# Loading the conditioning vector first, and two gate feature tiles beside the second chunk's norm

## The chip, the cores and the metric

The kernel runs on one core of a Trainium2 chip. Times are microseconds (us) of the device for one execution of the whole program. The names of the engines follow the profile: PE is TensorE (matmuls and transposes), PEld its weight loads, DVE is VectorE, ACT is ScalarE, POOL is GpSimd, and SP (SPq in the rows) is the queue from which every DMA of this kernel is issued.

## The reference

Two layers of a transformer-like block work on 1024 latent tokens and 256 context tokens of width 1024, all in float32. What matters here is the beginning of each layer:

```
shift, scale, gate = split(silu(c) @ w_mod[l] + b_mod[l], 3)        # latent; the context has its own from c_ctx
h  = rms_norm(x, norm_gain[l]) * (1 + scale) + shift
hc = rms_norm(ctx, norm_gain[l]) * (1 + scale_c) + shift_c
aq, ak, av, ag, bz, bg, nq, nk, nv, ng = split(h @ w_in[l], ...)     # widths 512,128,128,512,256,256,256,256,256,256
y = concat([attention(aq, ak, av) * silu(ag),
            pooling(bz) * silu(bg),
            neighbourhood_attention(nq, nk, nv) * silu(ng)]) @ w_out[l]
x = x + gate * y
```

The vector `c` and the learned vector `c_ctx` give, through the modulation weights `w_mod`, a shift and a scale for every one of the 1024 features. Only with these can a row of `x`, once normalized, be made into `h`, and only `h` can be multiplied by `w_in`. `ag` is the gate of the large attention: 512 features, that is four feature tiles of 128.

## The kernel before, in words

**Tiles.** Tokens come in chunks: tokens 0 to 511, 512 to 1023, and the 256 context tokens. `h` is kept transposed (features on the partitions) as a sum of a rounded part and a rest, `hh` and `hl`, each 128 x 8 x 1280. Weights are split in the same way into `wh` and `wl`, so one product of a 128-feature block takes three matmuls (hi by hi, hi by lo, lo by hi), and a feature tile of 512 tokens takes 8 x 3 = 24 matmuls (`feat_step`, L423 to L428; `proj_feat`, L430).

**The steps of a chunk.** `h_norm` (L234) squares the rows of a chunk on ScalarE, forms 1/rms, and scales the rows on VectorE. The squares themselves are of no use (only their sums are), and are written to a place that is free at the time: columns of `hl` that belong to the context, at L241. `h_steps` (L263) then gives eight steps, one for each block of 128 features: PE transposes up to four 128 x 128 tiles into a PSUM bank, ScalarE applies scale and shift and writes `hh`, GpSimd subtracts the shift again, and VectorE writes the rest to `hl`, reading the same bank. The steps lie in a list, `todo`, and `fill(n)` issues the next n of them at the place where it is called.

**Banks.** Three banks, `ps_b`, are handed out in turn by `ps_one` (L125): to the steps, to the small products of the modulation, and to some feature tiles. One bank, `ps_c`, is for the modulation rows. Four more, `ps_w`, hold the accumulators of feature tiles in this stage.

**The opening of layer 0.** The order of the DMAs is: identity and mask, the four row tiles of the first chunk (`x0`, L305, 512 KB each), the small rows of `c`, `c_ctx`, norm gain and modulation bias (`vrow`, L309), a selection matrix, and the first block of modulation weights (`mod_load`, L313, two transfers of 512 KB). Then comes a loop over j (L514). In round j, as far as j allows, the weight tile of the pooling branch for block j (256 KB) and the modulation weights of block j+1 are loaded; in rounds 2 to 5 also one row tile of the second chunk (`x1`, L519). PE computes the modulation of block j (`mod_rows`, L321), the columns of block j-1 (`mod_set`, L331), the first chunk's step for block j-1, and, three rounds behind, the four feature tiles of the pooling branch for block j-3. In rounds 4 to 7 the second chunk's rows are squared, and in round 7 scaled; its steps are issued two at a time in the last rounds, as are the loads and the norm of the context.

**Behind the loop.** The first chunk's four feature tiles leave their banks (`pool_in`), the second chunk's four tiles are computed with up to three context steps behind each of them (L564 to L567; the fourth takes its accumulator from `ps_one`), then the context chunk's tiles. The stages for the other columns of `w_in` follow, and last before the attention the gate stage (L716 to L740 and L805): weights of `ag`, two tiles for the context, and eight feature tiles (four features by two chunks), each multiplied with its SiLU (`silu_to`: three ScalarE passes and one VectorE product) and stored to `agd` in DRAM, from where the attention fetches it much later.

**What sets the order.** TensorE's instructions run in the order of the code. The order on the other engines and on the DMA queue is laid by the framework from the dependences; every wait on a buffer or a bank is set by it too.

Of the kernel before, what the change touches and what calls it, by code (L numbers as in the profile page):

```python
# [7 lines left out]
F32 = mybir.dt.float32  # L8
F32R = mybir.dt.float32r
BF16 = mybir.dt.bfloat16  # L10
AF = mybir.ActivationFunctionType
# [5 lines left out]
P = 128  # L17
D = 1024
# [56 lines left out]
def hybrid_block_kernel(  # L75
# [46 lines left out]

    ps_pair = ps_bank = ps_wide

    def ps_one(name):  # L125
        wide.b += 1
        return ps_b[wide.b % 3]

    def ps_acc(name):
        return ps_c  # L130
# [100 lines left out]
    def rows3(t):  # L231
        return t.rearrange("p (k c) -> p k c", c=P)

    def h_norm(n, hp=None):  # L234

        ss = small.tile([P, 4], F32, tag="lnss", name="lnss")
        xts, outs = [], []

        def add(xt):

            o = rows3(hp.tile([P, D], F32, name="xn", bufs=4)) if hp else hl[:, :, NTL * P:(NTL + 1) * P]  # L241
            i = len(xts)
            xts.append(xt)
            outs.append(o if hp else xt)
            ACT.activation(out=o, in_=xt, func=AF.Square, accum_out=ss[:, i:i + 1])

        def done():
            vv = small.tile([P, 4], F32, tag="lnv", name="lnv")
            DVE.tensor_scalar(out=vv[:, :n], in0=ss[:, :n], scalar1=1.0 / D, scalar2=EPS, op0=ALU.mult, op1=ALU.add)
            y = rsqrt(vv[:, :n], n, "ln")  # L250
            for i, xt in enumerate(xts):
                DVE.tensor_scalar(out=outs[i], in0=xt, scalar1=y[:, i:i + 1], scalar2=None, op0=ALU.mult)
            return outs

        return add, done

    def h_norm_all(xts):
        add, done = h_norm(len(xts))
        for xt in xts:
            add(xt)  # L260
        return done()

    def h_steps(l, t0, xns, hp, tname="htmp"):  # L263
        n = len(xns)
        v = 0 if t0 < NTL else 1
        w = n * P

        def step(k):
            ps = ps_one("ps_ht")
            for i in range(n):  # L270
                PE.transpose(ps[:, i * P:(i + 1) * P], xns[i][:, k, :], ident)
            a, b, nb = acol[:, l, v, k:k + 1], bcol[:, l, v, k:k + 1], nbcol[:, l, v, k:k + 1]
            dst = hh[:, k, t0 * P:t0 * P + w]
            ACT.activation(out=dst, in_=ps[:, :w], func=AF.Identity, scale=a, bias=b)
            tmp = hp.tile([P, 512], F32, name=tname, bufs=2)
            POOL.tensor_scalar(out=tmp[:, :w], in0=dst.bitcast(F32), scalar1=1.0, scalar2=nb, op0=ALU.mult, op1=ALU.add)
            DVE.scalar_tensor_tensor(out=hl[:, k, t0 * P:t0 * P + w], in0=ps[:, :w], scalar=a, in1=tmp[:, :w],
                                     op0=ALU.mult, op1=ALU.subtract)

        return [lambda k=k: step(k) for k in range(KT)]  # L280
# [19 lines left out]
    def load_x(t0, n, tiles):  # L300
        for i, xt in enumerate(tiles):
            SP.dma_start(out=xt, in_=rows3(x_rows(t0 + i)))
        return tiles

    x0 = load_x(0, 4, [rows3(pm.tile([P, D], F32, name="xt", bufs=8)) for _ in range(4)])  # L305
    vrow = pm.tile([40, P], F32, name="vrow")
    for r, v in ((0, c[0]), (8, c_ctx), (16, norm_gain[0]), (24, b_mod[0, 0:2 * D])):
        v = v.rearrange("(k p) -> k p", p=P)
# [4 lines left out]
    def mod_load(j):  # L313

        blk = stg.tile([P, KT, 256], F32, name="wmod", bufs=4)
        for i in range(2):
            SP.dma_start(out=blk[:, :, i * P:(i + 1) * P],
                         in_=w_mod[0, :, i * D + j * P:i * D + (j + 1) * P].rearrange("(k p) c -> p k c", p=P))
        return blk
# [18 lines left out]
        DVE.tensor_scalar(out=nbcol[:, 0, :, j], in0=bcol[:, 0, :, j], scalar1=-1.0, scalar2=None, op0=ALU.mult)  # L338

    blocks = [mod_load(0)]  # L340
    ps = ps_one("ps_v")
    PE.transpose(ps[:, 0:40], vrow, ident[0:40, 0:40])
    vcol = pm.tile([P, 40], F32, name="vcol")
# [30 lines left out]
    for l in range(DEPTH):  # L374
# [16 lines left out]
        def fill(n=1):  # L391
            for _ in range(n):
                if todo:
                    todo.pop(0)()

        def load_w_tile(cols, k):

            wh = wp.tile([P, 512], F32R, name="wh", bufs=9)
            wl = wp.tile([P, 512], F32R, name="wl", bufs=9)
            raw = wp.tile([P, 512], F32, name="wraw", bufs=4)  # L400
            o = 0
            for c0, w in cols:
                SP.dma_start(out=raw[:, o:o + w], in_=w_in[l, k * P:(k + 1) * P, c0:c0 + w])
                o += w
            split_w((wh, wl), raw[:, :o], slice(0, o))
            return wh, wl
# [30 lines left out]
        def silu_to(dst, ps, n, s=None):  # L437
            s = s or wp.tile([P, 512], F32, name="sig", bufs=2)
            sigmoid(s[:, :n], ps)
            DVE.tensor_tensor(out=dst, in0=ps, in1=s[:, :n], op=ALU.mult)  # L440


        ntok = SEQ if last else NT
        L = ntok + (24 if last else 32)
# [44 lines left out]
        if l:  # L489

            W = early_w + [load_w_tile([(C_BZ, 512)], k) for k in range(2, KT)]
            banks = []
            for i in range(2):
                pr = ps_pair("ps_feat")
                banks += [pr[:, 0:512], pr[:, 512:1024]]
            for i in range(2):
                for k in range(2):
                    for f in (2 * i, 2 * i + 1):
                        feat_step(banks[f], W, k, f, 0, 512)
            for k in range(2, KT):  # L500
                for f in range(4):
                    feat_step(banks[f], W, k, f, 0, 512)
                if k > 3:
                    fill(2)
            oprx.close()
            prex.close()
            W[:2] = [load_w_tile([(C_BZ, 512)], k) for k in range(2)]
        else:
            W = []

            banks = [ps_bank("ps_feat") for _ in range(4)]
            rows = None
            x1 = [rows3(pm.tile([P, D], F32, name="xt", bufs=8)) for _ in range(4)]
            for j in range(KT + 4):  # L514
                if j < KT:
                    W.append(load_w_tile([(C_BZ, 512)], j))
                    if j + 1 < KT:
                        blocks.append(mod_load(j + 1))
                    if 2 <= j < 6:  # L519
                        load_x(2 + j, 1, x1[j - 2:j - 1])  # L520
                    nxt = mod_rows(blocks[j])
                if 1 <= j <= KT:
                    mod_set(j - 1, rows)
                    first_h[j - 1]()
                if j == 4:
                    add1, done1 = h_norm(4)
                if 4 <= j < 8:
                    add1(x1[j - 4])
                if j == 7:
                    todo += h_steps(0, 4, done1(), wp, "sig")  # L530
                if j == KT:
                    SP.dma_start(out=edge, in_=k_edge)
                    x2 = load_x(NTL, 2, [rows3(pm.tile([P, D], F32, name="xt", bufs=8)) for _ in range(2)])
                if j == KT + 2:
                    todo += h_steps(0, NTL, h_norm_all(x2), wp, "sig")
                rows = nxt
                if j > KT:
                    fill(2)
                if 3 <= j < KT + 3:
                    for f in range(4):  # L540
                        feat_step(banks[f], W, j - 3, f, 0, 512)
            stx.close()
        lay = ExitStack()
        lp = lay.enter_context(pool(f"lay{l}", side=left))
        if l:
# [12 lines left out]
            DVE.memset(zt[:, :, 24 + NT:32 + NT], 0.0)  # L558
        for f in range(2):
            pool_in(f, 0, 512, banks[f])  # L560
        fill(2)
        for f in range(2, 4):
            pool_in(f, 0, 512, banks[f])
        for t0, n in chunks[1:2]:  # L564
            for f in range(4):
                pool_in(f, t0, n, proj_feat(W, f, t0, n, ps_one if l or f == 3 else None))
                fill(3)  # L567
# [8 lines left out]
        if l:  # L576
            use_banks("one")
        if l == 0:
            pmx.close()
            modp = pmx.enter_context(pool("modp", side="right"))  # L580
            todo += mod_part(0, 2 * D, modp, 2)
            for c0 in (0, D, 2 * D):
                todo += mod_part(1, c0, modp, 2)
            todo.append(lambda: mod_cols(1))
# [139 lines left out]
            silu_to(g, ps, 512)  # L724
            SP.dma_start(out=agc[t - NTL], in_=g)

        def gate_out(ps, f, t0, n, s=None):
            g = s or wp.tile([P, 512], F32, name="gate", bufs=2)
            silu_to(g, ps, 512, s)
            SP.dma_start(out=agd[f, :, t0:t0 + n], in_=g)  # L730

        def gate_feat(f, t0, n):
            gate_out(proj_feat(W, f, t0, n, ps_one if f == 3 else None), f, t0, n)

        gates = [lambda t=t: gate_tok(t) for t in range(NTL, ntq)]
        gates += [lambda f=f, t0=t0, n=n: gate_feat(f, t0, n) for f in range(4) for t0, n in chunks[:2]]
        for g in gates[:2]:
            g()
            lag.tick()
# [596 lines left out]
```

## Time and profile before

| | us |
|---|---|
| three runs | 1535.93, 1538.0, 1540.02; median 1538.0 |
| the profiled execution | 1539.72 |
| its span | 1537.9 |
| mean granted TensorE clock | 0.996 of full |
| TensorE busy | 1474.2 (96%) |
| VectorE busy | 860.2 (56%) |
| ScalarE busy | 637.6 (41%) |
| GpSimd busy | 513.1 (33%) |
| moved by DMA | 167.91 MB |

Rows of the timeline give the start of an instruction, or of several like it, from the start of the span; its length; the engine; the line of the kernel; the operation; the tile written and the tiles read; the shapes; how many; and in square brackets the idle time before it and what ended it. A matmul's length is from its start to its end in a pipeline, so that lengths overlap: what matmuls cost is read from start to start. Rows of a table of windows give the stretch, its length, for PE, PEld, DVE, ACT and POOL the busy us and the number of instructions, then the granted clock, the share of the DMA engines and GB/s. A wait list names who waited for whom: in total, how often, the longest.

### The profile page before, as it was taken

Reading aid. Unit: us, or ns where it says so; the run is one execution under the profiler, and the core shown is the slowest. Engines: PE = TensorE matmul, PEld = TensorE weight load, DVE = VectorE, ACT = ScalarE, POOL = GpSimd, SP = SyncE. Lnnn points to the kernel's source line nnn. Section 1 sums busy time; section 2 is a strip of 40 time slices with the busy share of each in tenths; the row PEclk is TensorE's granted clock in tenths of the full one; section 3 lists DMA queues with packets and bytes.
Section 4 is the critical chain, followed back from the end, with each engine's and each line's share of the span. In section 5 each row is a group of like instructions: output and inputs, shape, how many; then the busy total and the mean of one; then the engine's idle time right before and its main releaser. Section 6 shows DMA issues by size and latency. Waiting matters only on the chain.

```text
span 1537.9 us, 22259 instructions
## 1 busy us (share of the span) xinstructions
PE 1474.2 (96%) x8001; PEld 1072.8 (70%) x8001; DVE 860.2 (56%) x1666; ACT 637.6 (41%) x1220; POOL 513.1 (33%) x630
## 2 busy tenths in 40 slices
PE   5999999999999999998999999999998999999999
PEld 3787777788888555553788888878787854544577
DVE  3645234552678678875533543464358868786522
ACT  4543132333676444444312452332466544444400
POOL 0232336000134556565001233460013265565300
PEclk9999999999999999999999999999999999999999
DMA  9436455537745200101413222243697301001331
GB/s 317 140 97 219 133 158 162 165 107 192 178 113 159 73 27 25 39 8 55 168 58 109 76 93 91 85 142 82 155 227 172 89 21 42 21 24 39 133 121 55
DMA packets 153039, 167.91 MB, mean 109 GB/s; under 512 B 35384, under 2 KB 112032, under 8 KB 152864
## 3 DMA queue, kind: packets, MB, share of 16 engines
q1 hardware_dynamic: 152928, 166.48, 37.0%
q8 instruction: 63, 1.03, 0.3%
q14 instruction: 48, 0.39, 0.1%
HBM read 126.45 MB, written 40.86 MB: 109 GB/s over the span
## 4 chain that ended last, share of the span: by engine, by line
PE 80%; DVE 8%; ACT 4%; DMA 3%; issue 3%; SPq 1%; POOL 0%; DVEq 0%; POOLq 0%; ACTq 0%
PE ps_w L418 8%; PE ps_w L419 8%; PE ps_w L420 8%; PE ps_c L1049 8%; PE ps_w L1204 4%; PE ps_w L1207 4%; PE ps_w L1205 4%; PE ps_w L1029 4%; PE ps_b L1003 4%; PE ps_w L1030 3%; PE ps_c L894 3%; PE ps_b L882 2%; PE ps_w L426 2%; PE ps_w L428 2%; PE ps_w L427 2%
## 5 line engine op out<-in xcount | busy, mean ns | idle before, releaser
L1032 ACT ACTIVATE gp<-ps_w 128x1024 f32<-128x1024 f32 x160 | 162.4, 1022 | 190.9 <-PE ps_w L1030 155.3
L418 PE MATMUL ps_w<-wh,hh 128*128 128x512 f32 (+1 forms) x624 | 235.7, 378 | 2.2 <-ACT wh L287 2.2
L419 PE MATMUL ps_w<-wl,hh 128*128 128x512 f32 (+1 forms) x624 | 229.0, 367 | 1.0 <-DVE wl L288 1.0
L420 PE MATMUL ps_w<-wh,hl 128*128 128x512 f32 (+1 forms) x624 | 228.4, 366 | 0.0
L1004 DVE TENSOR_REDUCE gmx<-ps_b 128x1 f32<-128x512 f32 x256 | 171.7, 685 | 73.2 <-PE ps_b L1003 69.0
L1049 PE MATMUL ps_c<-gp,av 128*64 128x512 f32 x640 | 165.0, 609 | 10.3 <-ACT gp L1032 10.3
L1040 POOL TENSOR_TENSOR gacc<-gacc,gp 128x1024 f32<-128x1024 f32 x64 | 161.4, 2548 | 25.8 <-ACT gp L1032 25.5
L418 PEld LDWEIGHTS ps_w<-wh,hh 128*128 128x128 f32 x624 | 118.4, 190 | 27.8 <-issue 4.0
L419 PEld LDWEIGHTS ps_w<-wl,hh 128*128 128x128 f32 x624 | 117.8, 189 | 21.3 <-DVE wl L288 2.2
L420 PEld LDWEIGHTS ps_w<-wh,hl 128*128 128x128 f32 x624 | 117.6, 188 | 21.3
L1030 PE MATMUL ps_w<-gq,kst 128*128 128x512 f32 x320 | 126.7, 396 | 0.0
L1204 PE MATMUL ps_w<-woh,hh 128*128 128x512 f32 x272 | 109.5, 403 | 0.0
L1205 PE MATMUL ps_w<-wol,hh 128*128 128x512 f32 x272 | 107.4, 395 | 0.0
L639 DVE TENSOR_REDUCE qss<-sq 128x8 f32<-128x512 f32 (+2 forms) x58 | 31.1, 537 | 135.7 <-ACT sq L637 135.7
L1049 PEld LDWEIGHTS ps_c<-gp,av 128*64 128x64 f32 x640 | 42.5, 136 | 87.3 <-issue 65.2
L1037 POOL TENSOR_TENSOR gacc<-gp 128x1024 f32<-128x1024 f32 x32 | 75.8, 2369 | 50.0 <-ACT gp L1032 50.0
L288 DVE TENSOR_TENSOR wl<-wraw,wh 128x512 fp32r<-128x512 f32 (+1 forms) x96 | 66.3, 707 | 38.8 <-ACT wh L287 37.4
L1207 PE MATMUL ps_w<-woh,hl 128*128 128x512 f32 x272 | 85.6, 395 | 0.0
L426 PE MATMUL ps_w<-hh,wh 128*128 128x512 f32 (+1 forms) x208 | 81.6, 392 | 2.4 <-ACT wh L287 2.4
L866 ACT ACTIVATE prob<-ps_w,m 128x768 f32<-128x768 f32 (+2 forms) x88 | 72.7, 826 | 19.4 <-DVE m L853 7.4
L428 PE MATMUL ps_w<-hh,wl 128*128 128x512 f32 (+1 forms) x208 | 79.6, 382 | 0.0
L427 PE MATMUL ps_w<-hl,wh 128*128 128x512 f32 (+1 forms) x208 | 79.2, 381 | 0.0
(225 smaller groups left out, 2916.2 us busy)
## 6 DMA issues: line engine op xcount, KB each, us to landing
wmod<-in_w_mod_dram SPq DMA_DIRECT2D x48, 512.0 KB
wraw<-in_w_in_dram SPq DMA_DIRECT2D x64, 256.0 KB
gq<-qad SPq DMA_DIRECT2D x64, 128.0 KB
woraw<-in_w_out_dram SPq DMA_DIRECT2D x14, 512.0 KB
wraw<-in_w_in_dram SPq DMA_DIRECT2D x48, 128.0 KB
kst<-knd SPq DMA_DIRECT2D x16, 320.0 KB
qad<-qkhi SPq DMA_DIRECT2D x18, 256.0 KB
qad<-qklo SPq DMA_DIRECT2D x18, 256.0 KB
```

The costliest lines, as they stand in the source:

```text
L418: PE.matmul(ps[:, :n], a, wh[:, off:off + n], start=(k == 0), stop=False)
L419: PE.matmul(ps[:, :n], a, wl[:, off:off + n], start=False, stop=False)
L420: PE.matmul(ps[:, :n], b, wh[:, off:off + n], start=False, stop=(k == KT - 1))
L426: PE.matmul(ps[:, :n], wh[:, fs], hh[:, k, ts_], start=(k == 0), stop=False)
L1004: DVE.reduce_max(out=mx[:, qt, half:half + 1], in_=S, axis=AX.X)
L1030: PE.matmul(S[:, i, :], k2[:, kc], st.q2[hi], start=False, stop=True)
L1032: ACT.activation(out=p, in_=S, func=AF.Exp)
L1040: eng.tensor_tensor(out=st.acc[hi], in0=st.acc[hi], in1=pf, op=ALU.add)
L1049: PE.matmul(st.o[hi * 64:(hi + 1) * 64, :], av[:, kt, g * 64:(g + 1) * 64], st.p[hi, kp][:, i, :], start=(kt == 0), stop=(kt == NTT - 1))
L1204: PE.matmul(ps[:, i2, :], a, oh[:, cs], start=(k == 0), stop=False)
L1205: PE.matmul(ps[:, i2, :], a, ol[:, cs], start=False, stop=False)
L1207: PE.matmul(ps[:, i2, :], b, oh[:, i2 * 512:(i2 + 1) * 512], start=False, stop=(k == KT - 1))
```

## The change

- The small rows of the conditioning, the selection matrix and the first block of modulation weights are loaded ahead of the first chunk's rows.
- In the loop the modulation weights of block j+1 are issued ahead of the branch weights of block j. The second chunk's rows are no longer loaded in rounds 2 to 5: all four are issued in round 7, behind the last weights.
- Behind them, in round 7, the columns of `w_in` for gate features 0 to 255 are loaded (four transfers of 256 KB) and split; the two parts lie in the context columns of `hh` and `hl`, which the context's steps fill only later.
- The second chunk's squares are made in rounds 9 to 11 and written to a free block of the modulation weights; its scaling stands behind the loop. No steps are issued in the loop.
- Behind the loop two gate feature tiles (features 0 to 255, tokens 0 to 511) are computed in two of the three `ps_b` banks. The second chunk's eight steps are issued between their blocks, with the third `ps_b` bank and `ps_c` as their ring. The ring gets its three banks back after the context chunk's tiles.
- The context's norm stands behind these two gate tiles.
- The gate stage of layer 0 leaves out the two tiles. It loads the same weights as before.

```diff
+    wide.ring = ps_b
+
     def ps_one(name):
         wide.b += 1
-        return ps_b[wide.b % 3]
+        return wide.ring[wide.b % len(wide.ring)]
...
-        def add(xt):
+        def add(xt, at=None):
-            o = rows3(hp.tile([P, D], F32, name="xn", bufs=4)) if hp else hl[:, :, NTL * P:(NTL + 1) * P]
+            o = at if at is not None else rows3(hp.tile([P, D], F32, name="xn", bufs=4)) if hp else hl[:, :, NTL * P:(NTL + 1) * P]
...
-    x0 = load_x(0, 4, [rows3(pm.tile([P, D], F32, name="xt", bufs=8)) for _ in range(4)])
     vrow = pm.tile([40, P], F32, name="vrow")
...
     blocks = [mod_load(0)]
+    x0 = load_x(0, 4, [rows3(pm.tile([P, D], F32, name="xt", bufs=8)) for _ in range(4)])
...
             for j in range(KT + 4):
                 if j < KT:
-                    W.append(load_w_tile([(C_BZ, 512)], j))
                     if j + 1 < KT:
                         blocks.append(mod_load(j + 1))
-                    if 2 <= j < 6:
-                        load_x(2 + j, 1, x1[j - 2:j - 1])
+                    W.append(load_w_tile([(C_BZ, 512)], j))
+                    if j == KT - 1:
+                        load_x(4, 4, x1)
+                        for i in range(0, KT, 2):
+                            raw = wp.tile([P, 512], F32, name="wraw", bufs=4).rearrange("p (k c) -> p k c", k=2)
+                            SP.dma_start(out=raw, in_=w_in[l, i * P:(i + 2) * P, C_AG:C_AG + 256].rearrange("(k p) c -> p k c", p=P))
+                            a, b = hh[:, i:i + 2, SEQ:NT], hl[:, i:i + 2, SEQ:NT]
+                            ACT.activation(out=a, in_=raw, func=AF.Copy)
+                            DVE.tensor_tensor(out=b, in0=raw, in1=a.bitcast(F32), op=ALU.subtract)
+                        G = [(hh[:, i, SEQ:NT], hl[:, i, SEQ:NT]) for i in range(KT)]
                     nxt = mod_rows(blocks[j])
                 if 1 <= j <= KT:
                     mod_set(j - 1, rows)
                     first_h[j - 1]()
-                if j == 4:
-                    add1, done1 = h_norm(4)
-                if 4 <= j < 8:
-                    add1(x1[j - 4])
-                if j == 7:
-                    todo += h_steps(0, 4, done1(), wp, "sig")
                 if j == KT:
                     SP.dma_start(out=edge, in_=k_edge)
                     x2 = load_x(NTL, 2, [rows3(pm.tile([P, D], F32, name="xt", bufs=8)) for _ in range(2)])
-                if j == KT + 2:
-                    todo += h_steps(0, NTL, h_norm_all(x2), wp, "sig")
+                    add1, done1 = h_norm(4)
+                    room = stg.tile([P, KT, 256], F32, name="wmod", bufs=4)
+                if j > KT:
+                    for i in ((0,), (1,), (2, 3))[j - KT - 1]:
+                        add1(x1[i], room[:, :, i % 2 * P:(i % 2 + 1) * P])
                 rows = nxt
-                if j > KT:
-                    fill(2)
                 if 3 <= j < KT + 3:
                     for f in range(4):
                         feat_step(banks[f], W, j - 3, f, 0, 512)
             stx.close()
+            todo += h_steps(0, 4, done1(), wp, "sig")
+            wide.ring = [ps_b[0], ps_c]
...
         for f in range(2):
             pool_in(f, 0, 512, banks[f])
-        fill(2)
+        if l:
+            fill(2)
+        else:
+            for f in range(2):
+                for k in range(KT):
+                    feat_step(ps_b[1 + f], G, k, f, 0, 512)
+                    if f or k > 3:
+                        fill()
         for f in range(2, 4):
             pool_in(f, 0, 512, banks[f])
+        if not l:
+            for f in range(2):
+                gate_out(ps_b[1 + f], f, 0, 512)
+            todo += h_steps(0, NTL, h_norm_all(x2), wp, "sig")
         for t0, n in chunks[1:2]:
...
         if l == 0:
+            wide.ring = ps_b
...
-        gates += [lambda f=f, t0=t0, n=n: gate_feat(f, t0, n) for f in range(4) for t0, n in chunks[:2]]
+        gates += [lambda f=f, t0=t0, n=n: gate_feat(f, t0, n) for f in range(4) for t0, n in chunks[:2]
+                  if l or f > 1 or t0]
```

The function `gate_out` (L727) is moved up without a change of its own, so that it can be called here.

More of the change, by code (lines that the diff above doesn't have):

```diff
@@ L440, in silu_to, with gate_out @@
             DVE.tensor_tensor(out=dst, in0=ps, in1=s[:, :n], op=ALU.mult)
+        def gate_out(ps, f, t0, n, s=None):
+            g = s or wp.tile([P, 512], F32, name="gate", bufs=2)
+            silu_to(g, ps, 512, s)
+            SP.dma_start(out=agd[f, :, t0:t0 + n], in_=g)
         ntok = SEQ if last else NT
@@ L725, in gate_tok @@
             SP.dma_start(out=agc[t - NTL], in_=g)
[L727 to L730, printed above, removed]
         def gate_feat(f, t0, n):
```

## The prediction

> **What bounds the kernel now.** I read the page first, then the early windows, then the waits of TensorE, then the rows of each engine around the two places that the change touches.
>
> ```profile
> span 1537.9 us, 22259 instructions
> PE 80%; DVE 8%; ACT 4%; DMA 3%; issue 3%; SPq 1%; POOL 0%; DVEq 0%; POOLq 0%; ACTq 0%
> ```
>
> The chain that ended last is TensorE for four fifths of the span, and TensorE runs in the order in which the code is written. So an edit is worth what it takes from, or adds to, TensorE's waits; a matmul that only moves is worth nothing. The waits of TensorE in the first 130 us, from two answers (up to 60 us, and 60 to 130 us), in total, times, longest:
>
> ```profile
> PE ps_c L326 <- DVE csel L352: 4.8, 1, 4.8
> ```
>
> ```profile
> PE ps_b L271 <- DVE hl L277: 1.4, 2, 0.8
> ```
>
> The first is the wait for the conditioning vector, the second the two short waits at the end of the second chunk's steps (a step: transpose into a bank, scale on ScalarE, subtract on GpSimd and VectorE). Behind those steps TensorE is full until the first chunk's rows of the whole branch are done (busy us of 26.00 in the second column of numbers):
>
> ```profile
> 68.00:94.00 26.00, 26.00 (x130) 21.52 (x129) 8.14 (x17) 12.69 (x23) 4.75 (x10) 1.00 0.14 45
> ```
>
> So 1.35 us of waits are to be had after the opening, and whatever the opening itself gives. I go through the change in that order.
>
> **The opening: conditioning first.** The sync queue, ScalarE's weight splits, and TensorE:
>
> ```profile
> 3.56 0.37 SPq L309 DMA_DIRECT2D vrow<-in_c_dram  x1
> ...
> 5.00 0.42 SPq L311 DMA_DIRECT2D sel<-in_k_sel_dram  x1
> 6.58 2.82 SPq L317 DMA_DIRECT2D wmod<-in_w_mod_dram  x2
> ```
>
> ```profile
> 14.75 0.63 ACT L287 ACTIVATE wh<-wraw 128x512 fp32r<-128x512 f32 x1 [0.19 <-DMA wraw<-in_w_in_dram]
> ...
> 18.82 0.63 ACT L287 ACTIVATE wh<-wraw 128x512 fp32r<-128x512 f32 x1 [0.36 <-DMA wraw<-in_w_in_dram]
> ```
>
> ```profile
> 16.08 1.94 PE L326 MATMUL ps_c<-wmod,csel 128*32 128x256 f32 x16 [4.79 <-DVE csel L352]
> 18.52 1.94 PE L326 MATMUL ps_c<-wmod,csel 128*32 128x256 f32 x16 [0.50 <-ACT mrows L328]
> ...
> 22.28 1.94 PE L326 MATMUL ps_c<-wmod,csel 128*32 128x256 f32 x16
> ```
>
> ```profile
> 10.00:20.00 10.00, 3.72 (x33) 1.38 (x33) 4.41 (x14) 4.18 (x12) 0.00 (x0) 1.00 1.03 311
> 20.00:30.00 10.00, 10.00 (x65) 6.42 (x58) 4.25 (x13) 4.73 (x10) 1.38 (x2) 1.00 1.11 357
> ```
>
> At first sight 16.08 us is far too late, and with the vector loaded first the block at 16.08 can start when its weights land, near 9 us. But the second block is what counts, since nothing else is ready between. ScalarE waited for the raw weights themselves: the branch weights of block 0 landed at 14.7, of block 1 at 18.8, which is 1.31 MB (two 512 KB modulation transfers and a 256 KB one) in 4.1 us, about 320 GB/s, and the engines are saturated (share 1.03 and 1.11, 311 and 357 GB/s in the last column). The 256 KB go last, 0.8 us, so modulation block 1 landed near 18.0, only half a microsecond before its use at 18.52; one more 1.31 MB at 357 GB/s, 3.7 us, puts block 2 at 21.7 against 22.28. The old opening waits for the vector, but the transfers stand right behind it.
>
> After the change the 2 MB of rows still lie ahead of modulation block 1 (program order: vector, block 0, rows, block 1). Of what precedes block 1 only the 256 KB weight tile goes behind it: -0.8 us. Against this five small issues now precede every large one: 5.42 minus 3.56, +1.86 us. The 311 GB/s of 10 to 20 us against 357 of the next ten suggest a queue that was not kept full; making good 0.25 MB of it gives -0.8. Together +0.3 us; bounds are -1.0 (full rate from the start) and +1.8 (neither gain). Afterwards each block takes TensorE longer than its transfers (the second chunk's 2 MB now wait behind them), so the opening moves the rest by this much and no more. I take **+0.3**.
>
> **Gate products and the second chunk's steps.** The two accumulators take two of the three small banks; the steps get a ring of two, one of these and the modulation bank. What a bank costs is shown by a step of before, from its transposes to the last read:
>
> ```profile
> 65.99 0.66 PE L271 MATMUL ps_b<-ident,xt 128*128 128x128 f32 x4 [0.76 <-DVE hl L277]
> 67.24 0.66 PE L271 MATMUL ps_b<-ident,xt 128*128 128x128 f32 x4 [0.59 <-DVE hl L277]
> 67.65 0.48 PE L426 MATMUL ps_w<-hh,wh 128*128 128x512 f32 x1
> ...
> 73.35 0.82 PE L271 MATMUL ps_b<-ident,xt 128*128 128x128 f32 x6
> ```
>
> ```profile
> 66.69 0.78 ACT L274 ACTIVATE hh<-ps_b,bcol,acol 128x512 fp32r<-128x512 f32 x1 [0.41 <-PE ps_b L271]
> ...
> 69.08 0.60 ACT L190 ACTIVATE sig<-ps_w 128x512 f32<-128x512 f32 x1 [0.36 <-DVE hl L277]
> ...
> 70.82 0.62 ACT L192 ACTIVATE sig<-sig 128x512 f32<-128x512 f32 x1
> ```
>
> ```profile
> 68.29 0.75 DVE L277 SCALAR_TENSOR_TENSOR hl<-ps_b,acol,sig 128x512 fp32r<-128x512 f32 x1 [0.44 <-POOL sig L276]
> ```
>
> 65.99 to 69.04 (68.29 and 0.75): a bank is taken for 3.05 us. On TensorE a step costs 0.41 us (67.24 to 67.65) and a feature tile of 24 matmuls 5.70 (67.65 to 73.35), so three matmuls 0.71. Between a step and the next but one, which needs its bank, stand two steps and six matmuls, 2.24 us. Each later pair waits 0.8 us; eight steps have three later pairs: 2.4 us. Into the same stretch fall the SiLU chains of feature tiles 2 and 3 and of the first gate, three ScalarE passes each (0.60 for the first, 0.62 for the last, in the rows above), which share the two small "sig" buffers with the steps; each pass put in front of a step's scaling lengthens it by about 0.6. Bounds 2.0 and 6.0; I take **3.0**, nearest to the undisturbed chain. The two waits of before, **-1.35**, go. The products themselves, 11.4 us, are matmuls that leave the gate stage later.
>
> **Context steps with two banks.** This is where the ring is dearest, and the diff restores three banks only behind it. After feature tiles 0, 1 and 2 of the second chunk the code issues up to three steps in a row (3, 3, 2), and feature tile 3 takes its accumulator from the same ring:
>
> ```profile
> 79.61 0.81 PE L271 MATMUL ps_b<-ident,xt 128*128 128x128 f32 x6
> ```
>
> ```profile
> 80.31 1.47 ACT L274 ACTIVATE hh<-ps_b,bcol,acol 128x256 fp32r<-128x256 f32 x3
> ```
>
> ```profile
> 81.48 0.94 DVE L277 SCALAR_TENSOR_TENSOR hl<-ps_b,acol,sig 128x256 fp32r<-128x256 f32 x2 [4.55 <-POOL sig L276]
> ```
>
> Three steps went back to back in 0.81 us because three banks were free. The first bank is released when the first of the two VectorE operations ends, 81.95: 2.34 us after 79.61. With two banks the third step waits 2.34 less 0.54 for two steps, 1.8 us; twice; and feature tile 3 waits as long for the bank of step 7. Three times 1.8: **+5.4** (bounds 5.0 and 6.5). It has no cover: TensorE is the engine that waits, and its order is written out.
>
> **The context norm.** It moves from the last products of the opening to behind the gate products, because its squares write over the columns that hold the gate weights. From its first square to its last scaling it took before
>
> ```profile
> 58.84 1.06 ACT L245 ACTIVATE hl<-xt 128x1024 fp32r<-128x1024 f32 x1
> ```
>
> ```profile
> 63.87 1.41 DVE L252 TENSOR_SCALAR xt<-xt,rs_y 128x1024 f32<-128x1024 f32 x2
> ```
>
> 58.84 to 65.28, 6.4 us, and now only one feature tile, 5.70, covers it: 0.7 us of wait if the squares come first, 2.7 with a gate's SiLU chain (2.0) in front, none if it runs less disturbed than before. I take **+1.5**, bounds 0 and 2.7.
>
> **What I cost at nothing.** The four splits of the gate weights (0.6 us of ScalarE and as much of VectorE each) and their 1 MB lie under the last four blocks' products. The second chunk's rows are the end of some 14.7 MB, which at 350 GB/s from 5 us on land near 47, and are needed past 64; without that cover a norm of 6 us would show. Later, two products of 5.70 us leave the gate stage, so the attention starts sooner after the stores it reads; its bias tables are the last to be ready:
>
> ```profile
> 376.69 1.09 DVE L773 TENSOR_TENSOR ntab<-cmask,ntab 128x896 f32<-128x896 f32 x1 [0.99 <-DMA ntab<-rpbd]
> ...
> 394.80 0.75 DVE L853 CUSTOM_DVE_ANT_0 ps_w<-ps_w,ntab,m 128x512 f32<-128x512 f32 x1
> ```
>
> 17 us lie between, 6 remain. So the full 11.4 come back there, and they cancel the 11.4 above.
>
> **Sum.** 0.3 + 3.0 - 1.35 + 5.4 + 1.5 = +8.9 us. The profiled execution took 1539.7, giving 1548.6; it lies 1.7 above the median of the runs, 1538.0, so for a median **1547**. The bounds add to +5.7 less 1.0, and +15.7: main case 1542 to 1553.
>
> **Rivals.**
>
> *A: the opening pays in full, not slower.* If block 1 of the modulation weights isn't held by bandwidth, everything moves with block 0, from 16.08 to about 9: 7 us, and 1547 less 7.3 is 1540, no change that can be told. For it: TensorE's list has no wait on these weights at all. Against it: raw weights landed in step with their use. It decides from the point where block 1 lands before about 12 us.
>
> *B: the clock falls behind the new waits.* The trace shows what a gap can cost:
>
> ```profile
> 140.00:150.00 10.00, 8.59 (x42) 5.71 (x41) 5.58 (x11) 3.93 (x8) 0.00 (x0) 1.00 0.73 218
> 150.00:160.00 10.00, 9.06 (x39) 5.93 (x43) 1.81 (x7) 1.13 (x5) 6.13 (x11) 0.83 0.78 275
> ```
>
> 2.35 us of idle in pieces there, and then 0.17 of ten microseconds of clock, 1.7 us, was lost. If each of the three context waits does this: +5.1, 1552. Against it: the 1.35 us at 65 to 67 cost no clock. The Trainium skill, "TensorE: Matmul & The Clock Gate" (section "HAM oscillation — how this bites in real kernels"), names idle gaps above about 3.4 us as what throttles, by which B adds nothing and the sum stays; the row above, with no gap that long, does not agree. The section "A second HAM failure mode: psum-queue depth-cycling" of the same page tells of short waits between bank groups that throttle repeatedly, which is B.
>
> *C: SiLU first.* If ScalarE runs all four chains (two branch tiles, two gates, 2.0 each) after the gate products and before the context's squares, the context steps wait 8.0 + 6.4 - 5.7 = 8.7 instead of 1.5: 1554.
>
> **How the numbers follow.** Main case 0.60, A 0.15, B 0.12, C 0.10, the rest nothing named. About 0.3% is what a measurement can tell, 4.6 us: below 1533.4 is faster, above 1542.6 slower. A third of A (an opening that pays and milder waits) and a little else is faster: 0.07. The rest of A and the low end of the main case are the same: 0.20. Slower 0.73. The range, 1538 to 1555, takes in most of A's upper half, B and C.
>
> **What would show it.** Right: block 1's matmuls at 18 to 20 us although block 0's start near 9; three waits of TensorE on VectorE's `hl` of 0.8 us or so within the gate products; two waits of 1.8 at context steps and one ahead of feature tile 3; the gate stage 11 us shorter. Wrong: block 1 near 12 us; steps that follow each other on two banks without a wait; or the stall near 148 us gone, which I leave as it is.

## The result and the profile after

The changed kernel took 1548.06 us in the median of eleven runs, the kernel before 1538.0 on the same occasions: ratio 1.0061, 95% interval 1.0047 to 1.0075. Slower, and within 1.1 us of the forecast.

The profiled execution was one of the short ones (1542.02 us, span 1540.2, where the runs go from 1541.4 to 1553.0), so its span shows only 2.3 us of the 10. A second profile was therefore taken; its span is 1544.5. From the first gate product to the stage behind the branch the two agree (60.7 and 60.6 us); the openings differ by 2.6 us, and the rest of the 4.3 us between the spans comes later. I call them the first and the second profile after.

The opening, first profile after, timeline of TensorE (lines are two or so lower than before: L326 is now L327, L271 L273, L426 L428, L277 L279):

```profile
8.90 1.93 PE L327 MATMUL ps_c<-wmod,csel 128*32 128x256 f32 x16 [4.13 <-DMA wmod<-in_w_mod_dram]
17.68 1.93 PE L327 MATMUL ps_c<-wmod,csel 128*32 128x256 f32 x16 [6.85 <-DMA wmod<-in_w_mod_dram]
...
21.44 1.94 PE L327 MATMUL ps_c<-wmod,csel 128*32 128x256 f32 x16
...
28.20 0.47 PE L428 MATMUL ps_w<-hh,wh 128*128 128x512 f32 x1
```

Block 0 starts 7.2 us earlier, and nearly all of it is given back in a wait of 6.85 us for block 1, which starts at 17.68 instead of 18.52 (at 17.95 in the second profile after; in another profile of the kernel before it is 17.28, so the change doesn't bring block 1 forward for certain). The first branch product in the second profile after:

```profile
28.97 0.78 PE L428 MATMUL ps_w<-hh,wh 128*128 128x512 f32 x1
```

0.78 us for that matmul against 0.47, and the matmuls behind it start 0.43 us apart against 0.23: here TensorE still ran at half clock at the first branch product, as in the kernel before (0.78 us, 0.43 apart); in the first profile the full clock had come before it.

The gate products, first profile after, same view (the rows between are their matmuls):

```profile
59.66 0.40 PE L428 MATMUL ps_b<-hh 128*128 128x512 f32 x1
...
63.09 0.60 PE L273 MATMUL ps_b<-ident,xt 128*128 128x128 f32 x4
...
64.23 0.60 PE L273 MATMUL ps_c<-ident,xt 128*128 128x128 f32 x4
...
66.22 0.66 PE L273 MATMUL ps_b<-ident,xt 128*128 128x128 f32 x4 [0.69 <-DVE hl L279]
...
69.47 0.66 PE L273 MATMUL ps_b<-ident,xt 128*128 128x128 f32 x4 [0.76 <-DVE hl L279]
...
71.33 0.66 PE L273 MATMUL ps_c<-ident,xt 128*128 128x128 f32 x4 [0.51 <-DVE hl L279]
...
73.12 0.66 PE L273 MATMUL ps_b<-ident,xt 128*128 128x128 f32 x4 [0.44 <-DVE hl L279]
...
75.28 0.66 PE L273 MATMUL ps_c<-ident,xt 128*128 128x128 f32 x4 [0.81 <-DVE hl L279]
...
78.55 0.39 PE L428 MATMUL ps_w<-hh,wh 128*128 128x512 f32 x1
```

The steps take turns on a small bank and the modulation bank. Those with a bracket waited for VectorE's last read of their bank: five waits, 3.2 us, where the prediction had three. Then the context steps behind feature tiles 0 and 1, and feature tile 3:

```profile
84.15 0.38 PE L273 MATMUL ps_b<-ident,xt 128*128 128x128 f32 x2
84.37 0.38 PE L273 MATMUL ps_c<-ident,xt 128*128 128x128 f32 x2
86.61 0.44 PE L273 MATMUL ps_b<-ident,xt 128*128 128x128 f32 x2 [1.86 <-DVE hl L279]
...
94.89 0.44 PE L273 MATMUL ps_c<-ident,xt 128*128 128x128 f32 x2 [1.80 <-DVE hl L279]
...
103.17 0.50 PE L428 MATMUL ps_b<-hh,wh 128*128 128x512 f32 x1 [1.80 <-DVE hl L279]
```

Where before three steps stood in one row of 0.81 us, the third now stands alone behind 1.8 us. Both profiles have the same list here to 0.1 us; the second one's waits of TensorE from 60 to 115 us:

```profile
PE ps_b L273 <- DVE hl L279: 3.8, 4, 1.9
PE ps_c L273 <- DVE hl L279: 3.0, 3, 1.8
PE ps_b L428 <- DVE hl L279: 1.8, 1, 1.8
```

8.6 us on a list that held 1.4 before. How much it shifts the work is read at the first matmul of the stage behind (L418 before, L420 after): before, first and second profile after, one row from each:

```profile
103.43 0.28 PE L418 MATMUL ps_w<-wh,hh 128*128 128x256 f32 x1
```

```profile
120.38 0.28 PE L420 MATMUL ps_w<-wh,hh 128*128 128x256 f32 x1
```

```profile
122.85 0.28 PE L420 MATMUL ps_w<-wh,hh 128*128 128x256 f32 x1
```

48 gate matmuls now lie ahead of it, 11.0 us at 0.229 us from start to start (59.66 to 63.09 are 15 of them). So the shift that is loss is 5.9 us in the first profile and 8.4 in the second. The products come back in the gate stage: from this stage to the first scores of the attention it is 286.1 us in another profile of the kernel before (103.29 to 389.4) and 275.3 in the second after (122.85 to 398.2), 10.8 less. These two have waits of 1.5 and 1.9 us and full clock in that stretch. In the first pair it is 12.1 less (288.5 and 276.4), with waits of 2.35 us and 1.7 us of lost clock before, and waits of 2.9 us after.

```profile
L846 PE MATMUL ps_w<-kst,nq x100: 278/282/446, 389.4 to 1163.1; 128*128 128x256 f32 x84, 128*128 128x384 f32 x16
```

```profile
L867 PE MATMUL ps_w<-kst,nq x100: 278/282/446, 398.2 to 1170.7; 128*128 128x256 f32 x84, 128*128 128x384 f32 x16
```

### The profile page after: what moved, and what is told of

The parts are those of the page before. It is cut to its first block, busy times and chain, and to the rows that moved or that the text cites. A ratio compares the mean times of both kernels' runs of the same rounds, so it can differ in the third digit from the quotient of the medians.

```text
span 1540.2 us, 22278 instructions
## 1 busy us (share of the span) xinstructions
PE 1470.0 (95%) x8001; PEld 1069.3 (69%) x8001; DVE 861.8 (56%) x1670; ACT 641.0 (42%) x1224; POOL 513.3 (33%) x630
## 4 chain that ended last, share of the span: by engine, by line
PE 81%; DVE 8%; ACT 4%; DMA 3%; issue 3%; POOL 1%; SPq 1%; DVEq 0%; POOLq 0%; ACTq 0%
PE ps_w L420 8%; PE ps_w L421 8%; PE ps_w L422 8%; PE ps_c L1070 7%; PE ps_w L1225 4%; PE ps_w L1228 4%; PE ps_w L1226 4%; PE ps_w L1050 4%; PE ps_b L1024 4%; PE ps_c L915 3%; PE ps_w L1051 3%; PE ps_w L430 3%; PE ps_w L428 3%; PE ps_w L429 3%; PE ps_b L903 2%
## 5 line engine op out<-in xcount | busy, mean ns | idle before, releaser
L420 PE MATMUL ps_w<-wh,hh 128*128 128x512 f32 (+1 forms) x624 | 235.2, 377 | 1.3 <-ACT wh L289 1.3
L420 PEld LDWEIGHTS ps_w<-wh,hh 128*128 128x128 f32 x624 | 118.0, 189 | 26.5 <-issue 3.7
L662 ACT ACTIVATE sq<-ps_w 128x512 f32<-128x512 f32 (+2 forms) x58 | 27.9, 481 | 122.3 <-PE ps_w L422 122.3
L908 ACT ACTIVATE probt<-ps_b 128x512 f32<-128x512 f32 (+2 forms) x120 | 59.3, 522 | 41.0 <-PE ps_b L903 29.9
L428 PE MATMUL ps_w<-hh,wh 128*128 128x512 f32 (+1 forms) x192 | 73.4, 382 | 1.2 <-ACT wh L289 1.2
```

Of the source, the lines that this page charges most:

```text
L420: PE.matmul(ps[:, :n], a, wh[:, off:off + n], start=(k == 0), stop=False)
L428: PE.matmul(ps[:, :n], wh[:, fs], hh[:, k, ts_], start=(k == 0), stop=False)
```

## The experiments

Each ratio is against runs of the kernel before, taken in turn with it. The theory to test is that of the prediction, waits on a ring of two banks. The rivals are the clock that falls behind these waits (its case B), an opening that pays (A), and a loss elsewhere.

**The kernel before again.** No edit.

> The kernel before, unchanged, so that the granted clock of many of its executions can be read. Both theories: ratio 1.000. If new waits alone make the change slower, the mean clock here is about that of the changed kernel's eleven executions (0.992 to 0.998, middle 0.996). If cooling behind the new waits is a part of it, the clock here is higher on average, by some 0.002 for 3 us.

1538.14 us, ratio 1.0002 (0.9991 to 1.0013). The mean granted clock was 0.9942 over its 12 runs and 0.9946 over the 29 runs of the kernel before that were taken beside it; that of the changed kernel over its eleven is 0.9952. As time that the missing clock cost, one minus the clock times the time of each run, this is 8.3 us before and 7.5 us after. So the means show no clock lost by the change, but they can't settle a microsecond or two, because they count the opening unevenly. In the profile before, the clock column of the windows reads 1.00 from 20 to 40 us, although the first branch products (29.5 to 32.7 us) start 0.43 us apart, at half clock. In the profile of this run the full clock came at 19 us and was lost again in a wait of 3.07 us for block 3, and there the column shows it, 3.4 us from 20 to 40 us. What the new waits do to the clock is read in the windows below.

**The changed kernel again.** No edit.

> The changed kernel again, beside the other three, for a second profile: the first came from an execution at the low end (1542.0 of 1541.4 to 1553.0). The sum of the prediction says 1547 to 1548, ratio 1.006, with 8 to 9 us of waits on the ring in every execution and an opening that differs from one to the next. If the opening is what varies, block 1 or the first branch products start later here than 17.7 and 28.2 us; if something later varies, the gap to the kernel before opens behind 110 us.

1546.45 us, ratio 1.0057 (1.0045 to 1.0070), with the profile shown above. The lists of waits on the ring are the same to 0.1 us, and the 2.5 us between the two profiles at the stage behind are there when the gate products begin (59.66 in the first, 62.27 in the second): up to there it is the opening that varies, with the moment at which the full clock comes.

**Four banks behind the gate products.** The SiLU of the gates frees two of the three small banks; the steps may have them back at once.

```diff
             todo += h_steps(0, NTL, h_norm_all(x2), wp, "sig")
+            wide.ring = ps_b + [ps_c]
```

> The changed kernel, but behind the gate products and their SiLU the steps get four banks (three small ones and the modulation bank) instead of two. My theory (waits on the ring of two): the 1.86, 1.80 and 1.8 us of waits at the context steps and feature tile 3 go, 5.4 us, so about 1542 to 1543, ratio 1.003. If cooling behind these waits is a part: another 2 to 4 us, ratio 1.000 to 1.001. If the ring has nothing to do with it (loss elsewhere): 1548, ratio 1.006.

1542.03 us, ratio 1.0019 (1.0007 to 1.0032): 6 us of the 10 gone. The interval takes in my 1.003 and also the 1.001 that case B would give, so the time alone doesn't part the two. TensorE's waits from 60 to 115 us:

```profile
PE ps_b L273 <- DVE hl L279: 1.9, 3, 0.8
PE ps_c L273 <- DVE hl L279: 1.2, 2, 0.7
PE ps_b L273 <- DVE gate L442: 0.6, 1, 0.6
```

The three waits of 1.8 have left the list; those within the gate products stand, and one of 0.6 for a gate's SiLU has come. The mean clock, 0.9952, is that of the changed kernel.

**The gates in wide banks.** The two accumulators take the wide banks of branch tiles 0 and 1, and the ring stays at three small banks throughout.

```diff
-            wide.ring = [ps_b[0], ps_c]
...
+            gps = [ps_bank("ps_gate") for _ in range(2)]
-                    feat_step(ps_b[1 + f], G, k, f, 0, 512)
+                    feat_step(gps[f], G, k, f, 0, 512)
...
-                gate_out(ps_b[1 + f], f, 0, 512)
+                gate_out(gps[f], f, 0, 512)
```

> The changed kernel with the two gate accumulators in the wide banks that the branch tiles have just left, and the ring of three banks kept throughout. My theory: also the five waits within the gate products (3.2 us) go, 8.6 us in all, so 1539 to 1540, ratio 1.001; with an end to cooling behind them 1536, ratio 0.998. What is left is the opening and the old waits of 1.35 us, which the covered norm saves. If the gate products beside the steps cost in another way (ScalarE, the two small buffers): 1543 or more.

1538.26 us, ratio 1.0001 (0.9991 to 1.0012): the whole loss is gone, as far as can be measured. One wait is left, and what it drew behind it is seen at the first feature tile of the second chunk:

```profile
79.72 0.50 PE L428 MATMUL ps_w<-hh,wh 128*128 128x512 f32 x1 [2.23 <-DVE ub L442]
80.06 0.40 PE L429 MATMUL ps_w<-hl,wh 128*128 128x512 f32 x1
80.30 0.39 PE L430 MATMUL ps_w<-hh,wl 128*128 128x512 f32 x1
80.53 0.45 PE L428 MATMUL ps_w<-hh,wh 128*128 128x512 f32 x1
80.77 0.63 PE L429 MATMUL ps_w<-hl,wh 128*128 128x512 f32 x1
81.20 0.63 PE L430 MATMUL ps_w<-hh,wl 128*128 128x512 f32 x1
```

The tile wants the bank of branch tile 2, whose SiLU ScalarE took up only after the steps; and from 80.8 to 84.2 us the matmuls start 0.43 us apart instead of 0.23. That is the half clock, 1.7 us lost, about 1 us behind a wait of 2.23.

**SiLU first.** As the last, with the SiLU of branch tiles 2 and 3 ahead of the gate products in the code.

```diff
+            for f in range(2, 4):
+                pool_in(f, 0, 512, banks[f])
             gps = [ps_bank("ps_gate") for _ in range(2)]
...
-        for f in range(2, 4):
-            pool_in(f, 0, 512, banks[f])
+        if l:
+            for f in range(2, 4):
+                pool_in(f, 0, 512, banks[f])
```

> As the run with the gate accumulators in the wide banks, and the SiLU of branch tiles 2 and 3 stands ahead of the gate products in the code. There one wait was left, 2.23 us on the bank of branch tile 2, with the half clock behind it (1.7 us). If these are real costs, 1538.3 less 2.2 to 3.9: 1534.4 to 1536, ratio 0.9975 to 0.9985, faster than both kernels. If the steps are then late instead (ScalarE): 1538, ratio 1.000.

1534.82 us, ratio 0.9974 (0.9962 to 0.9985): faster than both kernels. From 20 to 115 us its list of TensorE's waits has one line:

```profile
PE ps_c L327 <- DMA wmod<-in_w_mod_dram: 0.9, 1, 0.9
```

Its gate products take, from their first matmul to the second chunk's first,

```profile
64.19 0.40 PE L428 MATMUL ps_w<-hh 128*128 128x512 f32 x1
```

```profile
79.05 0.39 PE L428 MATMUL ps_w<-hh,wh 128*128 128x512 f32 x1
```

14.86 us, where the changed kernel takes 18.89 (59.66 to 78.55). Two banks cost 4.0 us there. The move of the SiLU has no part in this: with the wide gate banks alone the gate products take 14.85 us (62.48 to their last matmul at 77.10, and 0.23 for it).

**TensorE kept busy in the waits.** Matmuls that nobody reads stand in the three long waits of the changed kernel.

```diff
-                fill(3)
+                if l:
+                    fill(3)
+                elif f < 3:
+                    fill(2)
+                    spare = wide.t[(wide.n + 1) % 4]
+                    for i in range(8):
+                        PE.matmul(spare, W[i][0][:, 0:P], hh[:, i, t0:t0 + n], start=True, stop=True)
+                    fill(1)
```

> The changed kernel with eight matmuls of 128x512 that nobody reads (1.9 us) put into each of the three waits at the context steps and feature tile 3, so that TensorE is busy where it waited; the waits as such stay. If only the waits cost: 1548, ratio 1.006, no change or a few tenths more. If the clock falls behind these waits in some executions: 2 to 5 us less, 1543 to 1546, and a mean clock of 0.997 or 0.998 in all executions.

1549.49 us, ratio 1.0076 (1.0059 to 1.0093), mean clock 0.9950. The first gap, filled; the step behind it no longer waits:

```profile
87.94 2.11 PE L597 MATMUL ps_w<-hh,wh 128*128 128x512 f32 x8
90.05 0.44 PE L273 MATMUL ps_b<-ident,xt 128*128 128x128 f32 x2
```

The filled gaps bring nothing, so case B falls as a price that every execution pays. In both profiles of the changed kernel these waits leave the clock alone; a table of windows of the second profile after, where the third column from the end is the granted clock:

```profile
80.00:90.00 10.00, 8.13 (x39) 6.45 (x38) 4.46 (x7) 8.48 (x15) 0.94 (x3) 1.00 0.14 53
90.00:100.00 10.00, 8.20 (x39) 6.45 (x39) 2.25 (x7) 2.19 (x5) 1.89 (x4) 1.00 0.00 0
100.00:110.00 10.00, 8.20 (x38) 6.46 (x37) 1.56 (x3) 2.64 (x5) 0.96 (x2) 1.00 0.40 117
```

1.8 us of idle in each ten, and full clock. The matmuls between the waits say the same, 0.23 us apart.

**The ring of two in the kernel before.** Everything else as before.

```diff
+    wide.ring = ps_b
+
     def ps_one(name):
         wide.b += 1
-        return ps_b[wide.b % 3]
+        return wide.ring[wide.b % len(wide.ring)]
...
             stx.close()
+            wide.ring = [ps_b[0], ps_c]
...
         if l == 0:
+            wide.ring = ps_b
```

> The kernel before with one edit: behind the opening loop, until the context chunk's tiles are done, the steps take turns on two banks (a small one and the modulation bank) instead of three. If the ring costs what its waits say: two waits of 1.8 us at context steps, one ahead of feature tile 3, and up to 0.8 us more at the last two steps of the second chunk, 5.4 to 6.5 us in all, ratio 1.0035 to 1.0042. If the ring only hurts beside the gate products: ratio 1.000.

1545.14 us, ratio 1.0044 (1.0032 to 1.0056), 6.8 us: two thirds of the loss or more, without any gate product. The same three waits (1.86, 1.80 and 1.80 us) are there:

```profile
73.70 0.47 PE L273 MATMUL ps_b<-ident,xt 128*128 128x128 f32 x2 [1.86 <-DVE hl L279]
...
83.52 0.44 PE L273 MATMUL ps_c<-ident,xt 128*128 128x128 f32 x2 [1.80 <-DVE hl L279]
...
91.79 0.49 PE L428 MATMUL ps_b<-hh,wh 128*128 128x512 f32 x1 [1.80 <-DVE hl L279]
```

With one of 0.75 at the second chunk's steps this makes 6.2 us of waits, 4.8 more than before. In this profile case B also happens once. Right behind the first of the three waits the matmuls start 0.43 us apart, up to 77.4 us:

```profile
73.89 0.71 PE L428 MATMUL ps_w<-hh,wh 128*128 128x512 f32 x1
74.40 0.63 PE L429 MATMUL ps_w<-hl,wh 128*128 128x512 f32 x1
74.83 0.63 PE L430 MATMUL ps_w<-hh,wl 128*128 128x512 f32 x1
```

The clock column gives 1.7 us lost there. So a wait of 1.86 us can be followed by the half clock, but of nine such waits, in this profile and the two of the changed kernel, this one alone was.

**The opening alone.** The kernel before with the new order of loads, the second chunk's rows where they were.

```diff
-    x0 = load_x(0, 4, [rows3(pm.tile([P, D], F32, name="xt", bufs=8)) for _ in range(4)])
...
     blocks = [mod_load(0)]
+    x0 = load_x(0, 4, [rows3(pm.tile([P, D], F32, name="xt", bufs=8)) for _ in range(4)])
...
-                    W.append(load_w_tile([(C_BZ, 512)], j))
                     if j + 1 < KT:
                         blocks.append(mod_load(j + 1))
+                    W.append(load_w_tile([(C_BZ, 512)], j))
```

> The kernel before with the order of the opening alone: conditioning and modulation block 0 ahead of the first chunk's rows, block j+1 ahead of the branch weights of block j; the second chunk's rows stay in rounds 2 to 5. My sum gave the opening +0.3 us (bounds -1.0 and +1.8): ratio 1.000. If the first start of TensorE near 9 us were worth its 7 us: ratio 0.9955. If the changed profile's 2.9 us were typical: ratio 0.998.

1539.07 us, ratio 1.0006 (0.9997 to 1.0014): nothing. Its first two blocks:

```profile
9.51 1.93 PE L325 MATMUL ps_c<-wmod,csel 128*32 128x256 f32 x16 [4.86 <-DMA wmod<-in_w_mod_dram]
18.50 1.94 PE L325 MATMUL ps_c<-wmod,csel 128*32 128x256 f32 x16 [7.06 <-DMA wmod<-in_w_mod_dram]
```

18.50 against 18.52 before. Case A falls.

**The best kernel with the old opening.** "SiLU first", with the rows ahead of the conditioning and the branch weights ahead of the modulation weights, as before.

```diff
+    x0 = load_x(0, 4, [rows3(pm.tile([P, D], F32, name="xt", bufs=8)) for _ in range(4)])
     vrow = pm.tile([40, P], F32, name="vrow")
...
     blocks = [mod_load(0)]
-    x0 = load_x(0, 4, [rows3(pm.tile([P, D], F32, name="xt", bufs=8)) for _ in range(4)])
...
+                    W.append(load_w_tile([(C_BZ, 512)], j))
                     if j + 1 < KT:
                         blocks.append(mod_load(j + 1))
-                    W.append(load_w_tile([(C_BZ, 512)], j))
```

> As the run with wide gate banks and SiLU first, but with the old opening: the first chunk's rows ahead of the conditioning, branch weights of block j ahead of modulation block j+1; the second chunk's rows stay behind them. If the opening's order is worth nothing, as the run of the opening alone says: ratio 0.9974 as with the new order, within 0.001. If conditioning first pays once the second chunk's rows are out of the way: 0.9985 or more.

1535.48 us, ratio 0.9990 (0.9977 to 1.0002). It overlaps both what was expected without worth and what was expected with it. Whether the order pays 2 us once the second chunk's rows are out of the way stays open.

**A warm opening.** "SiLU first" with matmuls that nobody reads behind modulation block 0.

```diff
                     nxt = mod_rows(blocks[j])
+                    if j == 0:
+                        for i in range(18):
+                            PE.matmul(banks[0][:, 0:256], ident, blocks[0][:, i % KT, :], start=True, stop=True)
```

> As the run with wide gate banks and SiLU first, and 18 matmuls of 128x256 that nobody reads behind modulation block 0, where TensorE waits 7 us for block 1. If the half clock up to the first branch products costs what it shows (in the profiles so far the full clock came between 19 and 36 us, by luck): 1.5 to 3 us less than 1534.8, ratio 0.9955 to 0.9965. If the opening is held by the transfers alone, or the clock falls again in the waits for blocks 2 and 3: ratio 0.9974, no change.

1533.94 us, ratio 0.9975 (0.9965 to 0.9985): no different from "SiLU first". In its profile the full clock is there from block 1 on, but the fillers run past the landing of block 1, which starts at 20.44:

```profile
20.44 1.07 PE L327 MATMUL ps_c<-wmod,csel 128*32 128x256 f32 x16
```

The first branch product starts at 26.66 us, against 30.41 in the profile of "SiLU first", and the stage behind the branch at 108.67 against 114.72. So 6.0 us are gained up to there, but the spans differ by 1.2 us only (1533.2 and 1534.4). The profiles show what took the rest: over windows of 20 us through the whole span, the clock column accounts for about 10.6 us lost here, all behind 150 us, and for about 5.2 in "SiLU first". The mean clock of all runs says the same, 0.9940 and 0.9963. Whether the earlier opening brings on these later spells of half clock or they fell so by chance isn't shown.

## Why the prediction was right, step by step

The sum was 8.9 us and the time 1547; measured were 10 us in the first comparison and 8 in the second (1548.06 and 1546.45). The mechanism is the one named, and it is shown from both sides: taken out of the changed kernel the loss goes (1.0061 to 1.0001), put into the kernel before it appears (1.0044). It also shows where the opening can't enter, from the first gate product to the stage behind the branch: 60.7 and 60.6 us in the changed kernel, 55.3 with four banks behind the gate products, 54.6 with the gates in wide banks, 50.5 with SiLU first. That the sum came so near is in part luck: two terms were too small, by 1.0 and 0.8 us, and one too large by 1.5. By term:

- **Opening, +0.3.** Right in kind: the transfers held block 1. Alone it measured 1.0006, +0.9 us with an interval of -0.5 to +2.2. Block 1 came at 17.68 and 17.95, just ahead of the 18 to 20 that I had named. What I had not seen is that the full clock comes at another moment in each execution, which moves the first branch products' end by 2 to 3 us between profiles of one kernel and made the first profile after look better than its median. Nor had I seen that the old opening too can wait for modulation weights: 3.6 us in the second profile of the kernel before, none in the one that I read.
- **Gate products, +3.0.** Undersized: 4.0 from start to start. The pair period of the rows was right for the first pair; later ones were longer because ScalarE put the context's squares between the steps (67.89 and 69.60, in the rows further below), and VectorE the scaling of a context row tile (73.81) ahead of the read that the last step waited for, not the SiLU chains that I had named. And a wait on the list is counted from the modelled end of the last matmul, which lies about 0.17 us behind the point where the next could have started (0.40 us long, 0.23 from start to start): five waits, 3.2 us listed, 4.0 paid.
- **Context steps, +5.4.** The waits are 1.86, 1.80 and 1.80, 5.5 us, each within 0.1 of the 1.8 worked out from the three rows of before. From the second chunk's first matmul to the next stage the changed kernel takes 41.8 us (78.55 to 120.38) and "SiLU first" 35.7 (79.05 to 114.72, its first row of that stage), so 6.2 in all, again a little above the listed waits.
- **Context norm, +1.5: wrong, it is 0.** The step that failed is "behind the gate products, because its squares write over the columns that hold the gate weights". They write over 128 columns of each block, those of the first gate tile, not of both. So they were free to run when the first tile's products were through, and ScalarE ran them between the steps:

```profile
67.89 1.05 ACT L247 ACTIVATE hl<-xt 128x1024 fp32r<-128x1024 f32 x1
...
69.60 1.05 ACT L247 ACTIVATE hl<-xt 128x1024 fp32r<-128x1024 f32 x1
```

(first profile after; the gate products end at 78.55.) The norm had a second gate tile more to hide under, and the price went into the longer steps above.

- **Old waits, -1.35.** Gone from the list, as said.
- **Costed at nothing.** The later gate stage gave back 10.8 of the 11.0 us. The splits and the second chunk's norm put no wait on TensorE's list.
- **Rivals.** A fell with the opening alone, B as a fixed price with the filled gaps and with the full clock between the waits of the changed kernel; a single spell of it stands in the profile of the ring of two in the kernel before. How often the changed kernel's executions have one isn't shown. In C, all four SiLU chains ahead of the context's squares on ScalarE were to be the dear case; the order that came was the reverse (all four chains behind the steps and the squares). What made the best kernel is another order, two chains ahead of the gate products. The 148 us stall that I left as it is differs from one execution to the next of the kernel before itself: 2.35 us and a lost clock in the profile shown, 1.5 us and full clock in the other. In the changed kernel its waits lie near 135 and 165 us, 2.9 us in the first profile and 1.9 in the second, at full clock.

The Trainium skill's rule that I set against B ("TensorE: Matmul & The Clock Gate", section "HAM oscillation — how this bites in real kernels": gaps above about 3.4 us throttle) agrees with the changed kernel, where gaps of 1.8 us in every 8 left the clock at 1.00. It does not agree with the run of the wide gate banks, where one wait of 2.23 us stood 1 us ahead of the half clock, nor with the 1.86 us right ahead of it in the ring of two, nor with the 2.35 us in pieces of the profile before. Its neighbour section on short waits between bank groups did not come true here: behind the five waits of 0.44 to 0.81 us the clock stayed at 1.00 (60 to 80 us).

## What to carry to other kernels

A ring of buffers has a price that can be read before anything is built: take the time from the writer's start to the last reader's end from one row each, subtract what the writer does until it needs the same buffer again, and the rest is a wait per turn; here 2.34 minus 0.54 gave 1.8, and 1.80 was measured. Before giving banks away for a long accumulation, look for others that are just being emptied: the wide banks were free, and what they cost was one wait of 2.23 us with the half clock behind it, until the SiLU of the bank wanted next was put first. And an engine that starts 7 us earlier gains next to nothing if its second input is due when it was; ask for the landing of the next one, not of the first.

## What the runs showed of the hardware that I had not expected

The moment at which TensorE reaches full clock in the opening is not fixed: the first branch matmul took 0.47 us in the first profile after and 0.78 in the second, of the same program. Over the twelve profiles it is 0.47 or 0.48 in five (the warm opening among them) and 0.78 in seven. Between the two profiles of the changed kernel this was worth 2.5 us at 120 us, more than most of the terms of the sum. With the moments at which the modulation weights land it spreads the start of the gate products over 6 us in the six profiles with the same opening (58.2 to 64.2). So a single pair of profiles says little about a change as small as this: the first pair of profiles (+2.3 us) would have given a quarter of the measured difference, and parts of two profiles are better compared from one instruction to another behind the opening.
